# Seven-product chunk pairs in both feed-forwards, with the weight sums chained in place

## Chip, cores and metric

The kernel runs on one core of one Trainium2 chip, as one program. The time is that of the device for one execution, in microseconds; before the change the median of three runs was 784.88 us (784.01 to 785.82).

The engines are named as in the profile: PE is TensorE, PEld its weight loads, DVE VectorE, ACT ScalarE, POOL GpSimd, SP the engine whose queue issues most transfers ("SPq").

## What is computed

One layer of a streaming encoder over 256 tokens of 1024 values: a feed-forward, a mixer with two branches, a memory read, and a second feed-forward. The change touches the two feed-forwards only:

```python
def swiglu(h, w_in, w_down):
    gate, up = jnp.split(h @ w_in, 2, axis=-1)
    return (jax.nn.silu(gate) * up) @ w_down

h = rmsnorm(x, ffn1_pre_g[l])
x = x + 0.5 * rmsnorm(swiglu(h, ffn1_w_in[l], ffn1_w_down[l]), ffn1_post_g[l])
...
h = rmsnorm(x, ffn2_pre_g[l])
x = x + 0.5 * rmsnorm(swiglu(h, ffn2_w_in[l], ffn2_w_down[l]), ffn2_post_g[l])
```

`w_in` is 1024 x 5632 (gate and up of 2816 each), `w_down` 2816 x 1024, all in float32.

## The kernel before

**Precision.** A float32 operand is split into hi, a cast to float32r by ScalarE (`S.copy`), and lo, the rest, by a subtraction on VectorE. A product is three matmul passes: hi by hi, hi by lo, lo by hi. So each weight unit (128 x 1024, 512 KB) is loaded by SP into a tile "raw" of a ring of four, cast by ScalarE and subtracted by VectorE into a hi and a lo tile of rings of eight (`load_split`, L136-L148).

**A feed-forward** (`ffn`, L419) cuts the 2816 hidden columns into 11 chunks of 256. Each has four units of `w_in`, of which each covers a quarter of the 1024 inputs and holds gate and up columns, and two units of `w_down`. The input projection of a chunk is done in one of three ways:

- by token (`act_tok`, `act_first`), chunks 0 and 1, and 2 in the first feed-forward: the tokens are the stationary operand, 128 at a time, and the result must be transposed afterwards (`flush`, L427: four transposes, then a split of the result)
- by column (`act_col`, L457), most of the others: 128 weight columns are stationary; 32 matmuls of 512 columns and 32 of 256 per chunk; no transpose. Its results go through banks "mm" and "tr" of two each
- as a pair of chunks (`act_pair`, L545), before the change only in the second feed-forward, chunks 5 and 6, and 9 and 10

**A pair** treats tokens (two blocks of 128), inputs (two halves of 512) and chunks (two) as a 2 x 2 by 2 x 2 block product, done with seven block products in place of eight. B00 to B11 are the weight blocks: first index the half of the inputs, second the chunk; each is two units. A block product (`product`, L562) is 12 matmuls of 512 columns. Sums of token blocks (`pair_inputs`, L506: de, aed, ad, baed, and e) are made once a feed-forward, after chunk 2; they need a row of per-token factors that POOL fetches through memory (`row_of`). Sums of weight blocks are made by VectorE in the weight tiles (`add`, L541-L543): B00 + B01, B11 + B01, and from these two more. Before, all eight tiles of a pair are loaded ahead (`raw_loads`, L533), four into the pool "m4" of 21 tiles and four into the pool "extra" of four; the order is b0, b0's second part, b2, b3, b4, b1, b4's second part. Both chunks of a pair need transposes.

**The down projection** of a chunk (`down`, L489) is done in two halves (row blocks of 128 tokens, h = 0 and 1) of 12 matmuls each, and lags behind: the loop at L691 does what is due after each chunk, `STAG` = 3 chunks are left for the end. In a pair, halves are set between the products by `step_between` (L569), from a list made at L658: in the second feed-forward four halves (chunks 3 and 4) in pair 5, none in pair 9.

**Order.** Each engine runs its instructions in the order of its queue. A planner sets the order when the kernel is built: by program order, changed by `tc.high_priority()`, by `tc.issue_after(i)` (behind instruction i) and by `after(n)` (behind the n-th matmul). Tiles of a pool come free when the last reader is done.

The tiles of "extra" also hold the mixer's first weights (`place`, L776-L777).

Of the kernel before, what the change touches and what calls it, by code (L numbers as in the profile page):

```python
# [11 lines left out]
F32 = mybir.dt.float32  # L12
# [6 lines left out]
P = 128  # L19
# [13 lines left out]

STAG = 3

PAIRS = {"f1_in": (), "f2_in": (5, 9)}

L_ACT = 21
L_F1 = 24
# [41 lines left out]
def block_kernel(ctx: ExitStack, tc: tile.TileContext, wts, head_in, gf_in, x_in, mem_in, memT_in, cols, rows, fbias, masks, out):  # L81
# [36 lines left out]
    def mm():  # L118
        return pp.tile([P, 512], F32, tag="mm", name=nm("mm"), bufs=2)
# [299 lines left out]
    def ffn(w_in, w_dn, X, r2, n_tok, i_row, first_half, second_half=None):  # L419
# [110 lines left out]
                out[n] = t  # L530
            return out, q

        def raw_loads(c, k, n):  # L533
            t = []
            for j in range(2):
                r = wp.tile([P, D], F32, tag="extra", name=nm("sraw"), bufs=4) if n else m4([P, D], n="sraw")
                loads.append(nc.sync.dma_start(r, wts[_AT[w_in] + 4 * (c + n) + 2 * k + j - 4]).ins)
                t.append(r)
            return t

        def add(t, o):  # L541
            for x, y in zip(t, o):
                V.tensor_tensor(out=x, in0=x, in1=y, op=ALU.add)  # L543

        def act_pair(c, between):  # L545
            sx, q = pairs_in

            def of(n):
                return lambda kk: (sx[n][:, 0, kk], sx[n][:, 1, kk])

            def of_x(k):
                return lambda kk: (X.hi(4 * k + kk, 0, P), X.lo(4 * k + kk, 0, P))

            def splits(t):
                u = []
# [4 lines left out]
                return u  # L560

            def product(ps, stat, u, start):  # L562
# [36 lines left out]
            product(b4, of("ad"), splits(B01), True)  # L599
            step_between()  # L600
            b1 = trp()
            product(b1, of("aed"), splits(B11), True)
            with tc.high_priority():
                V.tensor_tensor(out=v, in0=p1, in1=b1, op=ALU.subtract)
                V.tensor_tensor(out=w, in0=b3, in1=v, op=ALU.subtract)  # L605
                t = half_tile("c11")
                V.tensor_tensor(out=t, in0=w, in1=b4, op=ALU.subtract)
                act_evac(t, c + 1, 1, r2[0], q)
                t = half_tile("c01")
                V.tensor_tensor(out=t, in0=w, in1=p3, op=ALU.add)  # L610
                act_evac(t, c + 1, 0)
            step_between()
            product(b4, of("e"), splits(B10), False)
            t = half_tile("c10")
            V.tensor_tensor(out=t, in0=v, in1=b4, op=ALU.add)
            silu = act_evac(t, c, 1, r2[0], q)
            if c + 1 == NFF - 1:
                table(silu)
            while between:
                step_between()  # L620

        def pair_loads(c):
            if c in pairs and c not in raws:
                raws[c] = [raw_loads(c, k, n) for k, n in ((0, 0), (1, 1), (0, 1), (1, 0))]

        raws = {}
# [21 lines left out]
        for c in range(n_tok, NFF):  # L648
            if c - 1 in pairs:
                continue  # L650
            if c > 2 and c not in pairs:
                pair_loads(c + 1)
            if c in pairs:
                pair_loads(c)
            acts[c] = m4([P, 2, 2, T], F32R, "act")
            if c in pairs:
                acts[c + 1] = m4([P, 2, 2, T], F32R, "act")
                downs = [(i, h) for i in range(done, min(c, NFF - STAG - 1)) for h in range(2)]  # L658
                done = max(done, min(c, NFF - STAG - 1))

                def one(i, h):
                    n = len(log)
                    down(i, h)
                    if h == 1:
                        flush(n + L_ACT - 12)

                act_pair(c, [lambda i=i, h=h: one(i, h) for i, h in downs])
            elif c == 2 and first_half:
                n = len(log)
                (outs,) = act_first((c,), mm)  # L670
                for h in range(2):
                    flush(n + L_ACT + 24 * h)
                    act_evac(outs[h], c, h)
            else:
                n = len(log)
                up = act_col(c)
                flush(n + L_ACT)
                flush(n + L_ACT + 20)
                split(acts[c][:, 0], acts[c][:, 1], up)
            last = c + 1 if c in pairs else c  # L680
            if c <= 6 <= last:
                grow = load_row(i_row)
                if first_half:
                    with tc.issue_after(loads[-1]):
                        nc.sync.dma_start(masks_s, masks)
# [851 lines left out]
```

## Time and profile before

| | us |
|---|---|
| median of three runs | 784.88 |
| lowest, highest | 784.01, 785.82 |
| the profiled execution | 785.81 |
| its span, first to last instruction | 784.0 |
| granted TensorE clock, mean | 0.997 |

| engine | busy us | share of the span |
|---|---|---|
| PE | 771.9 | 98% |
| DVE | 598.6 | 76% |
| ACT | 479.6 | 61% |
| POOL | 15.8 | 2% |

A timeline row has the start, the length, the engine, the line, the operation, the tile written and those read, shapes and a count; in brackets the idle time before it and what ended it. Neighbouring like rows are merged, and consecutive ones overlap a little at their ends, so that the distance of two starts is the cost of one in a row. In a row of stretches the numbers are: length, then busy time and count of PE, PEld, DVE, ACT, POOL, the granted clock, the busy share of the transfer engines and GB/s. A group row has a count, the busy time and mean ns, and the idle time before. Every matmul has line 95, that of its helper, so matmuls are told apart by tile: "acc" with "act" is the down projection, "mm" or "tr" with "hlT" the input projection, "sx" a pair's product with a sum of token blocks, "sraw" a weight block of a pair.

### The profile page before, as it was taken

The numbers are of one execution on the slowest core, as the hardware profiler recorded it, in microseconds if no ns is written. First come the engines' busy times: TensorE is split into PE (matmuls) and PEld (weight loads), VectorE is DVE, ScalarE is ACT, GpSimd is POOL, SyncE is SP. The second block draws the span as 40 slices with busy tenths as digits, with TensorE's granted clock in tenths as the row PEclk, the third lists the DMA queues.
The fourth block names the chain that finished last, engine by engine and source line by source line (L and its number), as shares of the span: only waits on it lengthen the run. The fifth ranks groups of instructions, "written<-read, shape, count | busy, mean of one in ns | idle before, by whom it ended". The sixth has DMA issues, their size and how long they took to land.

```text
span 784.0 us, 12029 instructions
## 1 busy us (share of the span) xinstructions
PE 771.9 (98%) x4526; PEld 660.6 (84%) x4526; DVE 598.6 (76%) x948; ACT 479.6 (61%) x798; POOL 15.8 (2%) x39
## 2 busy tenths in 40 slices
PE   9999999999999999999999999999999999999996
PEld 7888888888888998898788888888888888888775
DVE  7766656677778899788776666885589599986994
ACT  7665544567775668557676345753668566655852
POOL 0000000000000101100000000000000000000000
PEclk9999999999999999999999999999999999999998
DMA  9766665463654535834676654455175736286031
GB/s 347 258 228 204 224 217 190 162 235 137 215 172 145 181 137 172 286 109 162 214 260 230 215 183 163 147 204 191 54 259 173 273 135 273 93 293 254 0 108 54
DMA packets 44505, 148.07 MB, mean 189 GB/s; under 512 B 5144, under 2 KB 8864, under 8 KB 44448
## 3 DMA queue, kind: packets, MB, share of 16 engines
q1 hardware_dynamic: 43168, 144.83, 52.4%
q0 software_dynamic: 848, 2.12, 1.1%
q8 instruction: 35, 0.57, 0.3%
q10 hardware_dynamic: 432, 0.37, 0.1%
q14 instruction: 22, 0.18, 0.1%
HBM read 146.24 MB, written 1.06 MB: 188 GB/s over the span
## 4 chain that ended last, share of the span: by engine, by line
PE 87%; DVE 6%; DMA 3%; ACT 2%; issue 1%; DVEq 0%; ACTq 0%; SPq 0%
PE acc L95 37%; PE mm L95 36%; PE tr L95 11%; DMA raw<-in_wts_dram 2%; DVE lo L147 2%; DVE lo L166 2%; ACT hi L145 1%; DVE sraw L543 1%; PE tr L377 1%; PE tr L436 1%; ACT p L1162 0%; DMA head<-in_head_dram 0%; PE tr L1174 0%; DVE mx L1160 0%; DVE p L1159 0%
## 5 line engine op out<-in xcount | busy, mean ns | idle before, releaser
L147 DVE TENSOR_TENSOR lo<-raw,hi 128x1024 fp32r<-128x1024 f32 (+1 forms) x236 | 280.2, 1202 | 61.9 <-ACT hi L145 47.0
L145 ACT CAST hi<-raw 128x1024 fp32r<-128x1024 f32 (+1 forms) x236 | 239.7, 1036 | 87.8 <-DMA raw<-in_wts_dram 40.4
L95 PE MATMUL mm<-hi,hlT 128*128 128x512 f32 (+1 forms) x512 | 153.9, 379 | 0.0
L95 PE MATMUL acc<-hi,act 128*128 128x512 f32 x352 | 112.0, 391 | 0.0
L95 PEld LDWEIGHTS mm<-hi,hlT 128*128 128x128 f32 x512 | 94.2, 188 | 15.9 <-ACT pc L583 0.3
L95 PE MATMUL mm<-lo,hlT 128*128 128x512 f32 (+1 forms) x256 | 95.7, 379 | 0.0
L95 PEld LDWEIGHTS acc<-hi,act 128*128 128x128 f32 x352 | 66.1, 188 | 14.0 <-ACT act L165 0.5
L95 PE MATMUL mm<-hlT,hi 128*128 128x512 f32 (+1 forms) x320 | 76.5, 371 | 1.0 <-DVE at L444 0.6
L95 PE MATMUL acc<-lo,act 128*128 128x512 f32 x176 | 69.0, 392 | 0.2 <-DVE lo L147 0.2
L95 PE MATMUL acc<-hlT,hi 128*128 128x512 f32 x272 | 68.4, 393 | 0.0
L95 PEld LDWEIGHTS mm<-hlT,hi 128*128 128x128 f32 x320 | 56.6, 189 | 10.4 <-DVE vw L605 0.9
L95 PE MATMUL tr<-hlT,hi 128*128 128x512 f32 x240 | 60.3, 392 | 0.0
L95 PEld LDWEIGHTS acc<-hlT,hi 128*128 128x128 f32 x272 | 48.9, 189 | 8.8
L95 PEld LDWEIGHTS mm<-lo,hlT 128*128 128x128 f32 x256 | 48.0, 188 | 7.5
L95 PEld LDWEIGHTS tr<-hlT,hi 128*128 128x128 f32 x240 | 43.1, 189 | 7.7
L95 PE MATMUL mm<-hlT,lo 128*128 128x256 f32 x288 | 45.9, 284 | 0.0
L95 PEld LDWEIGHTS mm<-hlT,lo 128*128 128x128 f32 x288 | 41.4, 190 | 2.7
L95 PEld LDWEIGHTS acc<-hlT,lo 128*128 128x128 f32 x272 | 37.3, 190 | 2.7
L95 PEld LDWEIGHTS acc<-lo,act 128*128 128x128 f32 x176 | 33.1, 188 | 6.8 <-DVE lo L147 0.6
L95 PE MATMUL acc<-hlT,lo 128*128 128x256 f32 x272 | 38.6, 283 | 0.0
L166 DVE TENSOR_TENSOR lo<-sraw,hi 128x1024 fp32r<-128x1024 f32 x28 | 32.9, 1218 | 4.4 <-ACT hi L165 4.4
L95 PEld LDWEIGHTS tr<-hlT,lo 128*128 128x128 f32 x240 | 32.8, 190 | 2.3
(291 smaller groups left out, 1151.3 us busy)
## 6 DMA issues: line engine op xcount, KB each, us to landing
raw<-in_wts_dram SPq DMA_DIRECT2D x231, 512.0 KB, 4.4
sraw<-in_wts_dram SPq DMA_DIRECT2D x16, 512.0 KB, 6.0
raw<-in_gf_dram SPq DMA_DIRECT2D x12, 344.0 KB, 3.8
head<-in_head_dram SPq DMA_DIRECT2D x7, 392.0 KB, 6.6
grow<-in_rows_dram SPq DMA_DIRECT2D x4, 512.0 KB, 6.2
xs<-in_x_dram SPq DMA_DIRECT2D x2, 512.0 KB, 7.8
cbm<-cd POOLq DMA_DIRECT2D x2, 512.0 KB, 8.9
brow<-in_rows_dram SPq DMA_DIRECT2D x4, 256.0 KB, 3.8
```

Source lines behind the costliest of these rows:

```text
L95: log.append(PE.matmul(*args, **kw).ins)
L145: S.copy(h, r)
L147: V.tensor_tensor(out=l, in0=r, in1=h.bitcast(F32), op=ALU.subtract)
L166: b = V.tensor_tensor(out=lo, in0=src, in1=hi.bitcast(F32), op=ALU.subtract)
L377: PE.transpose(blocks[-1][1], src(kb), ident)
L436: PE.transpose(trv[:, j, h * P : (h + 1) * P], ats[c, h][:, j * P : (j + 1) * P], ident)
L543: V.tensor_tensor(out=x, in0=x, in1=y, op=ALU.add)
```

## The change

- `PAIRS`: chunks 6 and 7, and 9 and 10, in both feed-forwards. The first had no pairs; the second had 5 and 6, and 9 and 10.
- Weight blocks: B00 and B01 are loaded ahead into the four tiles of "extra" (`sums` and `both`), each behind the loads of the chunk before; B11 and B10 come during the pair through the ring of four raw tiles. No tile of "m4" holds weights any more.
- The sums are chained in place: `sums` becomes B00 + B01, then + B11, then + B10; `both` becomes B01 + B11. There are eight additions of a tile, as before.
- The order of products is b0, b2, b3, b1, b0's second part, b4, b4's second part. b3 takes a bank of "tr" in place of "mm".
- Six places for down halves in a pair instead of five, and the down of chunk c - 2 is held back before a pair: pair 6 has the halves of chunks 3, 4 and 5, pair 9 those of chunk 6.
- The evacuations of a pair have high priority; the transposes of the chunk after a pair stand 24 matmuls later, and a second group 16 behind the first instead of 20.

The argument `op` of `more` is always `None`, and of `halves` only the first entry is read.

```diff
-PAIRS = {"f1_in": (), "f2_in": (5, 9)}
+PAIRS = {"f1_in": (6, 9), "f2_in": (6, 9)}
...
+        def sum_load(c, n, halves):
             t = []
             for j in range(2):
-                r = wp.tile([P, D], F32, tag="extra", name=nm("sraw"), bufs=4) if n else m4([P, D], n="sraw")
-                loads.append(nc.sync.dma_start(r, wts[_AT[w_in] + 4 * (c + n) + 2 * k + j - 4]).ins)
+                r = wp.tile([P, D], F32, tag="extra", name=nm("sraw"), bufs=4)
+                more(r, c, *halves[0], j, None)
                 t.append(r)
             return t
...
+        def more(r, c, k, n, j, op):
+            src = wts[_AT[w_in] + 4 * (c + n) + 2 * k + j - 4]
+            if op is None:
+                loads.append(nc.sync.dma_start(r, src).ins)
+            else:
+                G.dma_start(r, src, accum_op=op)
...
+            def raws(k, n):
+                t = [wp.tile([P, D], F32, tag="raw", name=nm("raw"), bufs=4) for _ in range(2)]
+                for j in range(2):
+                    more(t[j], c, k, n, j, None)
+                return t
...
-            B00, B11, B01, B10 = raws.pop(c)
-            b0 = mm()
-            product(b0, of_x(0), splits(B00), True)
-            add(B00, B01)
+            sums, both = sums_of_pair.pop(c)
...
+            b0 = mm()
+            product(b0, of_x(0), splits(sums), True)
             S.copy(p1, b0)
             step_between()
-            product(b0, of_x(1), splits(B10), False)
-            act_evac(b0, c, 0)
             b2 = trp()
-            u = splits(B11)
-            add(B01, B11)
-            add(B11, B00)
-            add(B10, B11)
-            product(b2, of("baed"), u, True)
+            raw = raws(1, 1)
+            product(b2, of("baed"), splits(raw), True)
             S.copy(p3, b2)
             step_between()
-            b3 = mm()
-            product(b3, of("de"), splits(B00), True)
-            step_between()
-            b4 = mm()
-            product(b4, of("ad"), splits(B01), True)
+            add(sums, both)
+            add(both, raw)
+            b3 = trp()
+            product(b3, of("de"), splits(sums), True)
+            add(sums, raw)
             step_between()
             b1 = trp()
-            product(b1, of("aed"), splits(B11), True)
+            product(b1, of("aed"), splits(sums), True)
             with tc.high_priority():
                 V.tensor_tensor(out=v, in0=p1, in1=b1, op=ALU.subtract)
                 V.tensor_tensor(out=w, in0=b3, in1=v, op=ALU.subtract)
+            step_between()
+            raw = raws(1, 0)
+            product(b0, of_x(1), splits(raw), False)
+            with tc.high_priority():
+                act_evac(b0, c, 0)
+            add(sums, raw)
+            step_between()
+            b4 = mm()
+            product(b4, of("ad"), splits(both), True)
+            with tc.high_priority():
...
-            product(b4, of("e"), splits(B10), False)
+            product(b4, of("e"), splits(sums), False)
...
+            if c in pairs and c not in sums_of_pair:
+                with tc.issue_after(loads[-1]):
+                    sums_of_pair[c] = sum_load(c, 0, ((0, 0), (0, 1))), sum_load(c, 1, ((0, 1), (1, 1)))
...
-            if c > 2 and c not in pairs:
-                pair_loads(c + 1)
...
-                flush(n + L_ACT)
-                flush(n + L_ACT + 20)
+                wait = 24 if c - 2 in pairs else 0
+                flush(n + L_ACT + wait)
+                flush(n + L_ACT + wait + 16)
                 split(acts[c][:, 0], acts[c][:, 1], up)
             last = c + 1 if c in pairs else c
+            if c > 2 and c not in pairs:
+                pair_loads(c + 1)
...
-            while done < (NFF - STAG if last == NFF - 1 else min(c - 1, NFF - STAG - 1)):
+            while done < (NFF - STAG if last == NFF - 1 else min(c - 1 - (c + 1 in pairs), NFF - STAG - 1)):
```

More of the change, by code (lines that the diff above doesn't have):

```diff
@@ L531, in pair_inputs @@
             return out, q
-        def raw_loads(c, k, n):
+        def sum_load(c, n, halves):
             t = []
             for j in range(2):
-                r = wp.tile([P, D], F32, tag="extra", name=nm("sraw"), bufs=4) if n else m4([P, D], n="sraw")
-                loads.append(nc.sync.dma_start(r, wts[_AT[w_in] + 4 * (c + n) + 2 * k + j - 4]).ins)
+                r = wp.tile([P, D], F32, tag="extra", name=nm("sraw"), bufs=4)
+                more(r, c, *halves[0], j, None)
                 t.append(r)
             return t
-        def add(t, o):
-            for x, y in zip(t, o):
-                V.tensor_tensor(out=x, in0=x, in1=y, op=ALU.add)
+        def more(r, c, k, n, j, op):
[4 more added lines that the diff above has]
+                G.dma_start(r, src, accum_op=op)
         def act_pair(c, between):
@@ L560, in splits, with add @@
                 return u
+            def raws(k, n):
[3 more added lines that the diff above has]
+                return t
+            def add(t, o):
+                for x, y in zip(t, o):
+                    V.tensor_tensor(out=x, in0=x, in1=y, op=ALU.add)
             def product(ps, stat, u, start):
@@ L612, in act_pair @@
             step_between()
-            product(b4, of("e"), splits(B10), False)
-            t = half_tile("c10")
-            V.tensor_tensor(out=t, in0=v, in1=b4, op=ALU.add)
-            silu = act_evac(t, c, 1, r2[0], q)
+            product(b4, of("e"), splits(sums), False)
+            with tc.high_priority():
+                t = half_tile("c10")
+                V.tensor_tensor(out=t, in0=v, in1=b4, op=ALU.add)
+                silu = act_evac(t, c, 1, r2[0], q)
             if c + 1 == NFF - 1:
@@ L622, in pair_loads @@
         def pair_loads(c):
-            if c in pairs and c not in raws:
-                raws[c] = [raw_loads(c, k, n) for k, n in ((0, 0), (1, 1), (0, 1), (1, 0))]
-        raws = {}
+            if c in pairs and c not in sums_of_pair:
+                with tc.issue_after(loads[-1]):
+                    sums_of_pair[c] = sum_load(c, 0, ((0, 0), (0, 1))), sum_load(c, 1, ((0, 1), (1, 1)))
+        sums_of_pair = {}
         pairs, pairs_in = PAIRS[w_in], None
```

## The prediction

> **What bounds the kernel now.** I read the page first (busy shares, then the chain that ended last), then the chain in order of time, then single engines over the two feed-forwards, called FF1 and FF2 below.
>
> ```profile
> PE 771.9 (98%) x4526; PEld 660.6 (84%) x4526; DVE 598.6 (76%) x948; ACT 479.6 (61%) x798; POOL 15.8 (2%) x39
> ...
> PE 87%; DVE 6%; DMA 3%; ACT 2%; issue 1%; DVEq 0%; ACTq 0%; SPq 0%
> ```
>
> TensorE is busy nearly all the time and holds 87% of the chain, so a change pays through TensorE's work or its pauses. The chain in order of time (start, length, what) gives the prices:
>
> ```profile
> 61.66 5.56 PE mm L95 x32
> 67.22 5.59 PE tr L95 x32
> 72.81 5.47 PE acc L95 x24
> 78.27 5.56 PE mm L95 x32
> ...
> 667.54 2.72 PE mm L95 x12
> 670.26 2.72 PE acc L95 x12
> ```
>
> In FF1 a chunk's input projection takes 72.81 - 61.66 = 11.15 us, its down projection (24 matmuls) 5.46, and the next follows without a pause. In FF2's pair a block product of 12 matmuls takes 2.72, a down half of 12 the same: 0.227 us a matmul. Four transposes add 0.44 us (44.61 - 43.94, less one matmul):
>
> ```profile
> 43.94 0.60 PE L436 MATMUL tr<-ident,at 128*128 128x128 f32 x4
> 44.30 0.48 PE L95 MATMUL acc<-lo,act 128*128 128x512 f32 x1
> 44.61 0.40 PE L95 MATMUL acc<-hi,act 128*128 128x512 f32 x1
> ```
>
> FF2 from its first pair on does pause. PE rows, its first and last matmul of that stretch and the longest pause:
>
> ```profile
> 667.38 0.39 PE L95 MATMUL mm<-hi,hlT 128*128 128x512 f32 x1
> ...
> 760.11 0.88 PE L436 MATMUL tr<-ident,at 128*128 128x128 f32 x6 [0.81 <-DVE at L444]
> ...
> 776.64 0.39 PE L95 MATMUL acc<-hi,act 128*128 128x512 f32 x1
> ```
>
> In between lie two pairs (168 matmuls), 16 down halves (192), two column chunks (22.30) and four groups of transposes (1.76): 360 x 0.2267 + 24.06 = 105.67 us. It took 776.64 + 0.23 - 667.38 = 109.49, so 3.8 us are pauses.
>
> VectorE, which makes every lo half and every weight sum, is the one that could take over (stretch, then busy time):
>
> ```profile
> 45.00:62.00 17.00, 17.00 (x92) 14.61 (x91) 12.42 (x16) 9.86 (x14) 0.00 (x0) 1.00 0.60 201
> 62.00:78.00 16.00, 16.00 (x87) 13.84 (x86) 9.88 (x13) 8.32 (x12) 0.00 (x0) 1.00 0.56 188
> 628.00:667.00 39.00, 39.00 (x207) 33.57 (x206) 38.38 (x52) 23.78 (x35) 0.00 (x0) 1.00 0.55 210
> 714.00:764.00 50.00, 48.60 (x225) 39.36 (x225) 44.16 (x50) 29.28 (x37) 0.00 (x0) 1.00 0.30 110
> ```
>
> The third number after the stretch's length is DVE: 12.42 of 17 in FF1, but 38.38 of 39 in FF2 where the pair is prepared, with TensorE still at 39.00. A full VectorE need not stop TensorE, but leaves nothing over.
>
> **FF1's two pairs, on TensorE.** Removed: two column chunks a pair, 22.30 us. Added: seven products, 19.04, and two groups of transposes, 0.88. Each pair saves 2.38, the two 4.76. FF2 keeps two pairs, so its work there stays and only its 3.8 us of pauses can shrink.
>
> **FF1's two pairs, on VectorE.** Prices:
>
> ```profile
> 741.85 8.02 DVE L166 TENSOR_TENSOR lo<-sraw,hi 128x1024 fp32r<-128x1024 f32 x7
> ...
> L543 DVE TENSOR_TENSOR sraw<-sraw,sraw 128x1024 f32<-128x1024 f32 x16 | 18.9, 1218 | 0.1
> ...
> 630.83 0.94 DVE L508 RECIPROCAL rho<-row 128x128 f32<-128x128 f32 x1
> ...
> 643.13 2.49 DVE L166 TENSOR_TENSOR sx<-ss,sx 128x512 fp32r<-128x512 f32 x4
> ...
> 49.04 0.42 DVE L219 TENSOR_TENSOR gate<-mm,plo 128x256 f32<-128x256 f32 x1
> ```
>
> A full-tile subtraction or sum costs 1.14 us in a row (8.02 over 7; the sums have the same mean of 1218 ns), a half-size one 0.6 (2.49 over 4), a quarter 0.33 (a row's 0.42 less the 0.08 by which neighbours overlap). A pair needs 14 lo's and 8 sums, 25.1; two chunks needed 8 lo's, 9.1. Evacuations fall from 6.3 (per chunk four quarters, three half-size) to 5.6 (five and two half-size, four quarter ones at about 0.4 less overlap). So each pair adds about 15.3 us. The stationary sums of L506-L530, new in FF1, are 15 half-size operations and 1.1 us of small ones: 10.1.
>
> **Where these 10.1 us fall.** They come after chunk 2, where FF1 has its weights just in time:
>
> ```profile
> 44.92 2.36 DVE L147 TENSOR_TENSOR lo<-raw,hi 128x1024 fp32r<-128x1024 f32 x2 [1.10 <-ACT hi L145]
> ```
>
> and on TensorE and POOL
>
> ```profile
> 44.84 2.01 PE L95 MATMUL mm<-hlT,hi 128*128 128x512 f32 x8
> 46.70 1.11 PE L95 MATMUL mm<-hlT,lo 128*128 128x256 f32 x8
> ...
> 26.14 0.57 POOL L356 DMA_DIRECT2D row<-rd x1 [1.73 <-DMA rd<-runs]
> ...
> row<-rd POOLq DMA_DIRECT2D x4, 128.0 KB, 5.5
> ```
>
> A column chunk needs its lo's 1.86 us after its start. From 44.9 to chunk 4's need (61.66 + 1.86 = 63.5) DVE has 18.6 us; due are two down lo's 2.3, the split of chunk 2's activations 0.6, chunk 3's evacuations 3.1 and chunk 4's lo's 4.6: 10.6, with the new work 20.7, 2.1 too much. The row that they need lands near 31.7 (26.14 + 5.5), so some can go into idle gaps before 44.9, and b2 of the pair, their first reader, comes near 94 us, so some can go later. FF2 took the same 10.1 us without a pause (38.38 of 39). If they stand ahead of chunk 3's lo's, about half (5.7) is late; if in the gaps, nothing. Between 0 and 5.7 I take 1.0, nearer FF2's row.
>
> **Pair 6 in either feed-forward.** TensorE: 19.04 + six halves 16.3 = 35.4 us. VectorE: 25.1 + six down lo's 6.8 + 5.6 + chunk 8's lo's 4.6 = 42.1, of which the first lo's, the first sum and B11's lo's (6.8) can run beside chunk 5: 35.3 in 35.4. With a half behind each product TensorE takes 5.44 a step. Before each product the demand, summed from the pair's start (down lo's, sums, product lo's), stays under the supply: 6.8 by b3 at 10.9, 13.7 by b1 at 16.3, 24 by b4 at 27.2. So no pause there, from 0 to the 0.81 of the row at 760.11: the last half (down 5, second row block) holds the transposes of chunk 7, nine matmuls (2.0 us) after that chunk's last subtraction can start, and the evacuation takes some 2.5. I take 0.5.
>
> **Pair 9.** Only down 6 is left to put between, so three products in a row (b3, b1, b0's second part) want 2 lo's and 2 sums each, 4.56 us of DVE against 2.72 of PE. Chunk 8 and the pair give TensorE 11.15 + 0.44 + 24.5 = 36.1 us; VectorE owes the pair's 25.1, down 6's 2.3, chunk 8's 3.1, a split of transposes 0.6 and the pair's evacuations before their transposes 4.0, in all 35.1, and about 1.2 of pair 6's evacuation. What stalls is what was not done beside chunk 8. Before, pair 9 with down 7 among its products ran 732.48 to 758.24, 25.76 for 24.5:
>
> ```profile
> 732.48 0.39 PE L95 MATMUL mm<-hi,hlT 128*128 128x512 f32 x1
> ...
> 749.83 1.07 PE L95 MATMUL acc<-hi,act 128*128 128x512 f32 x4
> ...
> 758.24 0.61 PE L95 MATMUL acc<-hi,act 128*128 128x512 f32 x2
> ```
>
> That is 1.3 of pause, the lower bound being 0, the upper 3 x (4.56 - 2.72) = 5.5, if nothing is done early. I take 1.5, next to the measured 1.3.
>
> **After pair 9.** Of the 3.8 us, 1.4 came behind 758.24 (72 matmuls and 0.88 of transposes from there would end at 775.45 instead of 776.87). ScalarE had the activation of chunk 10's first half behind a weight cast that waited for a transfer:
>
> ```profile
> 758.14 1.05 ACT L145 CAST hi<-raw 128x1024 fp32r<-128x1024 f32 x1 [2.48 <-DMA raw<-in_wts_dram]
> 759.10 0.50 ACT L441 ACTIVATE sg<-c,facs 128x256 f32<-128x256 f32 x1
> ```
>
> The new code raises these evacuations' priority, and they end before b4's second part. I take 0.3 (0 to 1.4).
>
> **Costed at nothing.** The second product into b4 must wait until DVE has read the first (0.6 us); a half covers it in pair 6, matmuls of down 7 in pair 9, as at 749.83; uncovered, about 1 us a pair. B11's and B10's loads now sit in SP's queue and in the ring of four raw tiles, B11 holding two through b3; behind them on SP wait the loads of downs 4 and 5 and chunk 8. In FF2 SP waits for a slot, not for bandwidth, and a sum's load lands 6.0 us after issue, against 5.4 us for each product with its half:
>
> ```profile
> SPq L143 <- DVE lo L147: 115.0, 33, 33.7
> ...
> sraw<-in_wts_dram SPq DMA_DIRECT2D x16, 512.0 KB, 6.0
> ```
>
> Without that cover one load late costs up to 6.0 less the work at hand. The flushes that move by a few matmuls change no count.
>
> **The sum.** FF1: -4.76 + 1.0 + 0.5 + 1.5 + 0.3 = -1.5. FF2: 0.5 + 1.5 + 0.3 - 3.8 = -1.5. Together -3.0. The profiled execution took 785.81 (span 784.0 and 1.8 around it), which becomes 782.8; it lies 0.93 above the median of 784.88, so the median becomes **781.9**.
>
> **Rivals.**
> *All hidden.* Every pause vanishes: -4.76 - 3.8, 776.3. For it: FF2's 39 us at a full VectorE. Against: pair 9 has no reserve.
> *VectorE takes over in pair 9* (slower). Each in-place sum waits for the lo's of the tile it overwrites, these for a free hi/lo pair, and that for TensorE; so nothing runs ahead. Per feed-forward 5.5, with 0.8 and 1.4 at their bounds and 1.0 in FF1: FF1 +3.9, FF2 +3.9, so 792.7. It decides once pair 9 loses more than 3.0 us in each, which takes DVE some 3 us behind at chunk 8's end.
> *FF1's stationary sums come first*: 5.7 for 1.0, 786.6.
> *The halves don't do what they are there for*: TensorE's order draws them ahead of the products, pair 6 meets the demand of pair 9, and some 3 us more over both give 784.9, no change. For it: down 7 slid between products at 749.83.
> *A pause long enough to lower the clock.* In the last row here TensorE has nothing to do and the granted clock falls to 0.64; eight warm-up matmuls (two records each) took 3.65 us before the first real one, against 0.09 for a transpose of that size:
>
> ```profile
> 777.00:784.00 7.00, 0.03 (x1) 0.00 (x0) 2.74 (x7) 1.54 (x5) 0.00 (x0) 0.64 0.22 75
> ...
> 0.79 3.65 PE L95 MATMUL tr<-const-float32-1.0 128*128 128x128 f32 x16 [0.79 <-PEq L1526]
> ```
>
> If pair 9's 5.5 came as one pause, a like stretch of 3.65 at about half speed adds 1.8 to the 792.7: 794.5. Nothing so far pauses over 0.81, and 714 to 764 shows a clock of 1.00. The Trainium skill ("TensorE: Matmul & The Clock Gate", What's actually happening) puts the fall to half clock at an idle window of about 3.4 us. By that rule the three shortfalls of 1.84, one by one, would not trip it; the last row's fall agrees with it, and no row here shows so long a pause inside the kernel.
>
> **How the numbers follow.** Forecast 0.40 (its own range 779 to 784), all hidden 0.13, VectorE 0.18, stationary sums 0.12, halves 0.14, clock 0.03. About 0.2% (1.6 us) can be told from no change, so faster is below 783.3, slower above 786.5. Faster: 0.38 + 0.13 + 0.02 of the halves = 0.53. Same: 0.02 + 0.10 + 0.05 of the stationary sums = 0.17. Slower: 0.18 + 0.03 + 0.07 + 0.02 = 0.30. Range 776 to 789: it leaves out the clock and most of the VectorE case.
>
> **What would show it.** The mixer's first matmul after FF1 starting 1 to 4 us earlier; pairs of 84 matmuls in both; a pause of 1 to 2 us in each pair 9, named after a lo or a sum. Wrong if chunk 4 in FF1 waits for lo's beyond 3 us, if pair 6 pauses more than pair 9, or if FF2 has more than 3.8 us of pauses.

## The result, and the profile after

The changed kernel takes 780.78 us (median of 4 runs, 779.74 to 781.5), the kernel before 785.24 (4 runs, 784.01 to 785.82): a ratio of 0.9944, 95% interval 0.9926 to 0.9962, so 4.5 us faster. The forecast was 781.9. The total is close to it, its parts are not, so that its closeness is in part luck. Three stretches of TensorE, told apart by the first matmul of FF1, of the mixer ("mm<-w") and of FF2 (again "mm<-w"), and by the end of the span. Their rows before:

```profile
189.58 2.88 PE L95 MATMUL mm<-w,hlT 128*128 128x512 f32 x12
...
268.00 0.72 PE L95 MATMUL acc<-qf,early 128*32 128x32 f32 x59 [1.28 <-issue]
...
593.10 2.88 PE L95 MATMUL mm<-w,hlT 128*128 128x512 f32 x12
```

And after:

```profile
4.26 1.59 PE L95 MATMUL acc<-hi,hlT 128*128 128x512 f32 x4
...
184.69 2.88 PE L95 MATMUL mm<-w,hlT 128*128 128x512 f32 x12
...
267.67 0.42 PE L95 MATMUL mm<-hi,hlT 128*128 128x344 f32 x1 [3.38 <-issue]
...
591.22 2.88 PE L95 MATMUL mm<-w,hlT 128*128 128x512 f32 x12
```

| profiled execution, us | before | after | difference |
|---|---|---|---|
| up to FF1's first matmul | 4.58 | 4.26 | -0.3 |
| FF1, to the mixer's first matmul | 185.0 | 180.4 | -4.6 |
| mixer, to FF2's first matmul | 403.5 | 406.5 | +3.0 |
| FF2, to the end of the span | 190.9 | 186.3 | -4.6 |
| span | 784.0 | 777.5 | -6.5 |
| the execution | 785.81 | 779.74 | -6.1 |

Both feed-forwards gained 4.6 us, and the mixer, of which the change touches no line, lost 3.0. (The profiled execution after is the fastest of its four, that of before the slowest of its first three, which is why 6.1 stands here and 4.5 above.)

The busy line, the chain and the whole list of TensorE's waits after:

```profile
PE 766.7 (99%) x4454; PEld 656.2 (84%) x4454; DVE 636.9 (82%) x989; ACT 490.4 (63%) x807; POOL 16.0 (2%) x39
...
PE 99%; issue 1%; DVE 0%; DVEq 0%; ACT 0%; ACTq 0%
```

```profile
PE mm L95 <- issue: 3.4, 1, 3.4
PE tr L95 <- PEq L1546: 0.8, 1, 0.8
```

TensorE now holds 99% of the chain, for 87% before. VectorE has 38 us more to do (598.6 to 636.9), and yet no wait for it is left: the one at 0.8 is the kernel's start, the one of 3.4 lies in the mixer and names no engine. TensorE's records fell by 72, 36 for each of FF1's pairs.

Around pair 9 of both feed-forwards, where the pauses were forecast (length, then busy time of PE, PEld, DVE, ACT, POOL, clock):

```profile
136.50:162.84 26.34, 26.34 (x117) 21.54 (x116) 26.31 (x29) 17.45 (x23) 0.00 (x0) 1.00 0.30 106
```

```profile
711.78:723.40 11.62, 11.62 (x69) 10.14 (x69) 11.19 (x16) 5.44 (x10) 0.00 (x0) 1.00 0.37 138
723.40:749.74 26.34, 26.34 (x116) 21.50 (x116) 26.31 (x29) 17.54 (x23) 0.00 (x0) 1.00 0.31 105
```

VectorE is full to 0.03 us, and TensorE is full as well. The chain in order of time shows how, in FF1's pair 9:

```profile
147.41 5.44 PE tr L95 x24
152.85 5.44 PE mm L95 x24
158.29 1.80 PE acc L95 x7
160.09 2.72 PE mm L95 x12
```

The seven "acc" at 158.29 are matmuls of down 7 that slid in ahead of the last product.

### The profile page after: what moved, and what is told of

Read it like the earlier page. It is cut to its first block, busy times and chain, and to the rows that moved or that the text cites. A ratio compares the mean times of both kernels' runs of the same rounds, so it can differ in the third digit from the quotient of the medians.

```text
span 777.5 us, 11945 instructions
## 1 busy us (share of the span) xinstructions
PE 766.7 (99%) x4454; PEld 656.2 (84%) x4454; DVE 636.9 (82%) x989; ACT 490.4 (63%) x807; POOL 16.0 (2%) x39
## 4 chain that ended last, share of the span: by engine, by line
PE 99%; issue 1%; DVE 0%; DVEq 0%; ACT 0%; ACTq 0%
PE mm L95 43%; PE acc L95 40%; PE tr L95 13%; PE tr L377 1%; PE tr L436 1%; PE tr L1194 0%; PE tr L1288 0%; PE acc L1407 0%; DVE xs L413 0%; DVE post L408 0%; DVEq L1552 0%; ACT junk L285 0%; DVE t L320 0%; PE tr L1045 0%; DVE y L322 0%
## 5 line engine op out<-in xcount | busy, mean ns | idle before, releaser
L147 DVE TENSOR_TENSOR lo<-raw,hi 128x1024 fp32r<-128x1024 f32 (+1 forms) x220 | 261.1, 1202 | 43.8 <-ACT hi L145 37.7
L145 ACT CAST hi<-raw 128x1024 fp32r<-128x1024 f32 (+1 forms) x220 | 223.7, 1035 | 76.2 <-PE mm L95 37.4
L95 PE MATMUL mm<-hi,hlT 128*128 128x512 f32 (+1 forms) x544 | 165.9, 382 | 3.4 <-issue 3.4
L95 PE MATMUL mm<-hlT,hi 128*128 128x512 f32 (+1 forms) x256 | 60.1, 365 | 0.0
L165 ACT CAST hi<-sraw 128x1024 fp32r<-128x1024 f32 x40 | 41.5, 1054 | 16.6 <-DVE sraw L573 10.7
L95 PEld LDWEIGHTS mm<-hlT,hi 128*128 128x128 f32 x256 | 44.9, 189 | 6.5
L166 DVE TENSOR_TENSOR lo<-sraw,hi 128x1024 fp32r<-128x1024 f32 x40 | 48.4, 1218 | 0.1
L95 PE MATMUL tr<-hlT,hi 128*128 128x512 f32 x176 | 44.6, 393 | 0.0
L95 PE MATMUL mm<-hlT,lo 128*128 128x256 f32 x224 | 36.6, 284 | 0.0
L95 PEld LDWEIGHTS tr<-hlT,hi 128*128 128x128 f32 x176 | 31.5, 189 | 5.6
```

The lines of the kernel that those rows point to most:

```text
L95: log.append(PE.matmul(*args, **kw).ins)
L145: S.copy(h, r)
L147: V.tensor_tensor(out=l, in0=r, in1=h.bitcast(F32), op=ALU.subtract)
L165: a = S.copy(hi, src)
L166: b = V.tensor_tensor(out=lo, in0=src, in1=hi.bitcast(F32), op=ALU.subtract)
```

## The experiments

Twelve kernels ran. For each, from its profiled execution: FF1 from its first down matmul ("acc<-hi,act") to the mixer's first, which leaves out the first 39 us with their uneven warm-up; the mixer; FF2 to the span's end; and the pause in the mixer that names no engine.

| run | median us | FF1 | mixer | FF2 | that pause |
|---|---|---|---|---|---|
| before | 785.24 | 150.7 | 403.5 | 190.9 | 1.28 |
| after | 780.78 | 146.1 | 406.5 | 186.3 | 3.38 |
| e1_ff2_only | 780.96 | 150.7 | 401.5 | 186.7 | none |
| e2_ff1_only | 785.78 | 146.6 | 405.5 | 190.7 | 2.63 |
| e3_shift72 | 777.99 | 147.2 | 404.1 | 186.3 | none |
| e4_shift36 | 783.42 | 146.6 | 407.3 | 186.3 | 3.74 |
| e5_shift72_short | 776.58 | 147.1 | 401.8 | 186.3 | none |
| e6_lo_twice | 787.95 (one run) | 150.4 | 406.9 | 188.8 | 2.82 |
| e7_no_hold | 786.44 | 149.4 | 406.4 | 190.0 | 2.85 |
| e8_no_priority | 781.51 | 146.4 | 406.7 | 186.6 | 3.24 |
| e9_old_pair | 797.01 | 154.9 | 403.8 | 201.2 | 1.77 |
| e10_before_short | 793.50 | 151.9 | 409.2 | 191.2 | 4.62 |
| e11_loads_first | 780.32 | 146.6 | 404.5 | 186.2 | 1.63 |
| e12_order_only | 786.13 | 149.5 | 406.1 | 188.9 | 2.35 |

The kernel before, run beside them, had medians of 785.2 (with e1 to e4), 784.8 (e5 to e8), 785.5 (e9 to e11) and 785.8 (e12). The stretches are read before the totals, since the mixer's pause changes with nearly every edit.

### Each feed-forward alone

```diff
-PAIRS = {"f1_in": (6, 9), "f2_in": (6, 9)}
+PAIRS = {"f1_in": (), "f2_in": (6, 9)}
```

> The changed code with no pairs in the first feed-forward (FF1), (6, 9) in the second (FF2). Theory A (read off the two traces): FF2 alone gives about 4.6 us, and the mixer, which then meets the same TensorE instructions ahead of it as before, keeps its pause of about 1.3 us near 267 us: 785.2 - 4.6, about 780.6, FF1 ending at about 189.6 us. Theory B (the prediction's sum): FF2 gives 1.5, so about 783.7.

```diff
-PAIRS = {"f1_in": (6, 9), "f2_in": (6, 9)}
+PAIRS = {"f1_in": (6, 9), "f2_in": ()}
```

> The changed code with (6, 9) in FF1 and no pairs in FF2. FF2 then has no pauses but 4.8 us more matmul work than with pairs, about what its pauses cost before (3.8 to 4.7). Theory A: FF1 ends 4.9 us earlier, and the mixer takes back 3 to 3.7 us in the pause near 264 us that names no waiting engine: about 783.5. Theory B: FF1 gives 1.5 and nothing is taken back later: 783.7, but with FF1 ending only 1.5 us earlier. The end of FF1 and the mixer's pause tell them apart.

FF2 alone: 780.96, ratio 0.9947 (0.9931 to 0.9964). Its FF2 is as short as after (186.7), FF1 as long as before (150.7), and the mixer has no pause, where Theory A had one of about 1.3 stay: its time of 780.6 came out near without that part of its reason. FF1 alone: 785.78, ratio 1.0004 (0.9989 to 1.002); FF1 is 4.1 shorter than before, but the mixer has a pause of 2.63 us and is 2.0 longer. So the feed-forwards gain separately, some 4 us each, and in the profiled execution the mixer takes back half of FF1's gain. The expectation of 783.5 for FF1 alone had counted such a loss already, and the profiled execution (783.87) is near it; the ten executions run from 782.74 to 787.77, and why their median is 2 us longer than the profiled one no trace shows.

### The same kernel with TensorE's instructions shifted

Extra warm-up matmuls ahead of everything move all that follows in TensorE's instruction stream, and change nothing behind them.

```diff
-    for _ in range(WARM):
+    for _ in range(5):
         MM(wps[:, :P], one, one, start=True, stop=True)
+    for _ in range(39):
+        MM(wps[:32, :32], one[:, :32], one[:, :32], start=True, stop=True)
```

> The changed kernel; of the eight warm-up matmuls before the first load lands, three are replaced by 39 small ones (128x32 by 32), so that TensorE's later instructions stand 72 matmul records (144 instructions with their weight loads) further on, as far as the kernel before had them. Theory A (the pause near 264 us comes where a block of TensorE's instructions ends inside the burst of small matmuls): the pause is 1.3 us again as before, the clock stays at 1.00, and the time falls by about 3 us to 777 to 778. Rival (the pause comes from transfers or from the earlier start of the mixer): it stays at 3.4 us and the time at 780.8.

```diff
-    for _ in range(WARM):
+    for _ in range(7):
         MM(wps[:, :P], one, one, start=True, stop=True)
+    for _ in range(19):
+        MM(wps[:32, :32], one[:, :32], one[:, :32], start=True, stop=True)
```

> As e3, with one warm-up matmul replaced by 19 small ones: 36 records (72 instructions) further on. Theory A: a pause of another length, between nothing and 3.4 us, at another matmul of the same burst, and a time between 776 and 781. Rival: pause 3.4 us at the same matmul, 780.8.

With 72 more records the pause is gone (Theory A had 1.3 us of it left), and the time is 777.99 us (0.9914, 0.9898 to 0.9929), although FF1 starts some 2 us later and the mixer waits 1.57 us for VectorE at another place (378.78). With 36 more the pause is 3.74 us and lies inside a burst of small matmuls, 783.42 us (0.998, 0.9969 to 0.9991), which is above the 776 to 781 of Theory A. The next run takes the 72 records without the later start:

```diff
-    for _ in range(WARM):
-        MM(wps[:, :P], one, one, start=True, stop=True)
+    for _ in range(44):
+        MM(wps[:32, :32], one[:, :32], one[:, :32], start=True, stop=True)
```

> The kernel after, with its 8 warm-up matmuls (16 records, 3.8 us) replaced by 44 of 32x32 (88 records, so again 72 more, but by 0.043 to 0.054 us a record only 3.8 to 4.7 us). Theory A (the mixer's pause of 3.38 us and the low clock behind it come from where the block of instructions ends, and the longer warm-up alone cost the run with 72 records its later start): no pause over 0.5 us near 265 us, the first matmul of FF1 at about 4.6 us and the mixer's at 184.7 to 185.5, and 776 to 777.5 us by the clock. Rival: small matmuls do not raise the clock in time, FF1 starts with matmuls at half speed, about 2 us lost, 778 to 779. Rival B (the pause follows the change itself, and it went with 72 records by the later start): the pause is back, 780.8.

**776.58 us**, 0.989 (0.9875 to 0.9904): the fastest of all, and 4.2 below the kernel after. Its window around the place of the pause, and that of the kernel after:

```profile
262.00:275.00 13.00, 13.00 (x263) 12.74 (x262) 12.38 (x25) 9.38 (x14) 2.66 (x12) 1.00 0.51 189
```

```profile
262.00:275.00 13.00, 9.62 (x105) 9.29 (x92) 7.79 (x17) 6.14 (x10) 2.65 (x12) 0.87 0.30 115
```

TensorE is busy all 13.00 us at a clock of 1.00, for 9.62 at 0.87. The mixer is 4.7 us shorter (406.5 to 401.8), though the pause was only 3.38: the rest went into matmuls at a lower clock, as rows of the kernel after show:

```profile
263.50 0.48 PE L95 MATMUL mm<-hi,hlT 128*128 128x344 f32 x2
263.81 0.32 PE L95 MATMUL mm<-lo,hlT 128*128 128x344 f32 x1
...
268.15 0.78 PE L95 MATMUL mm<-hi,hlT 128*128 128x344 f32 x2
268.73 0.49 PE L95 MATMUL mm<-lo,hlT 128*128 128x344 f32 x1
```

A pair took 0.31 us before the pause (263.81 - 263.50) and 0.58 behind it. The same shift was then given to the kernel before:

> The kernel before with the short warm-up matmuls (44 of 32x32 for 8 large ones, 72 more records). Theory A (the pause in the mixer is a matter of where a block of instructions ends, with or without the change): the pause of 1.28 us at 268 moves off the small matmuls or shrinks, mixer 401.5 to 402.5 us long for 403.5, and 782.5 to 783.5 us; the change is then worth 6 to 7 us, compared with 776.6. If the pause only moves to another matmul of the same burst: 784 to 786.5. Rival B (72 records help the kernel after alone): 784.8.

793.50 us, 1.0102 (1.0082 to 1.0123), against all that was expected: the pause did not shrink, it grew.

```profile
268.29 0.71 PE L95 MATMUL acc<-qf,early 128*32 128x32 f32 x59
273.62 0.32 PE L95 MATMUL acc<-qf,early 128*32 128x32 f32 x3 [4.62 <-issue]
```

The mixer lost 5.7 us (409.2 for 403.5); most of the rest is FF1, which started 0.9 later and had a pause of 1.03. So 72 records do not help as such: they took the pause away in one kernel and made it 3.3 us longer in the other. The place in the instruction stream bears on it (last section), but it is not all: the run with FF2's pairs alone comes to the mixer after as many records as the kernel before, and has no pause where that one has 1.28 us.

### VectorE's reserve

The first four lo's of one pair are computed twice: pair 9 in FF1, pair 6 in FF2.

```diff
                     split(p[0], p[1], r)
+                    if c == (9 if w_in == "f1_in" else 6) and dose:
+                        dose.pop()
+                        V.tensor_tensor(out=p[1], in0=r, in1=p[0].bitcast(F32), op=ALU.subtract)
                     u.append(p)
```

> The kernel after, with the first four lo's of one pair computed a second time (the same values; 4 x 1.14 = 4.6 us more of VectorE): in pair 9 of FF1, and in pair 6 of FF2. Theory A (VectorE has nothing left in pair 9, busy 26.27 of 26.30 us, and some 1.6 us in pair 6, busy 34.16 of 35.8): the mixer's first matmul moves from 184.7 to 188 to 189.3 with 3.5 to 4.6 us of pauses in pair 9, and FF2's pair 6 pauses by 2 to 3 us. Theory B (VectorE is merely kept full by work that it does ahead, and the down products slide in between): at most 1 us in pair 9 and none in pair 6.

FF1 is 4.2 us longer (150.4 for 146.1) for 4.6 us of work, FF2 2.5 (188.8 for 186.3). That is near Theory A at both places, in the one execution that there is, though less of it stands as a pause in the pairs than expected: 2.56 and 0.31 us in FF1's pair 9, 0.43 at the end of FF2's pair 6 and 0.80 and 0.33 behind it. The longest pause in FF1's pair 9 and the window over it:

```profile
156.79 0.39 PE L95 MATMUL mm<-hi,sx 128*128 128x512 f32 x1
159.74 0.50 PE L95 MATMUL mm<-lo,sx 128*128 128x512 f32 x1 [2.56 <-DVE lo L166]
```

```profile
157.00:160.00 3.00, 0.44 (x2) 0.26 (x2) 3.00 (x5) 2.71 (x4) 0.00 (x0) 1.00 0.69 212
```

Here TensorE has no down matmul to put in (the next stand at 162.37) and waits while VectorE is busy all 3.00 us. Taken as they are, 4.2 us for 4.6 leave pair 9 a reserve of 0.4 us; but FF1 varies from 146.1 to 147.2 us among the five kernels that differ only ahead of it or behind it (the kernel after, and the runs with FF1 alone and with shifted instructions), so the reserve is known to about a microsecond. Nor is all of a full VectorE need: in the kernel after, three lo's of later weights (L147, at 157.87, 160.20 and 161.74) are made inside the pair, and here they stand behind 164.21.

### The parts of the change, one by one

Without the hold-back:

```diff
-            while done < (NFF - STAG if last == NFF - 1 else min(c - 1 - (c + 1 in pairs), NFF - STAG - 1)):
+            while done < (NFF - STAG if last == NFF - 1 else min(c - 1, NFF - STAG - 1)):
```

> The kernel after, without the hold-back: chunk 8 and chunk 5 no longer keep a down product, so that pair 9 has none of the six second halves between its products and pair 6 fewer; the matmuls are the same. Theory A (the halves are what hides VectorE's 15.3 us in a pair): pauses of 1.5 to 4 us in each pair 9, the mixer's first matmul at 186 to 189, and 784 to 789 us. Theory B (VectorE works ahead on lo's, the order of the down products does not matter): no pause over 0.5 us in a pair, 780.8 us. The pause near 265 us stays either way.

786.44 us, 1.0018 (1.0005 to 1.003): the whole gain is gone. FF1 +3.2, FF2 +3.7. Its waits of TensorE, the longest first:

```profile
PE mm L95 <- issue: 2.8, 1, 2.8
PE mm L95 <- DVE c L633: 1.6, 2, 0.8
PE mm L95 <- DVE c L624: 0.8, 1, 0.8
...
PE mm L95 <- DVE at L444: 0.6, 1, 0.6
```

The pauses of 1.6 (two) and 0.8 name the pair's evacuations (c) and stand partly at the first matmuls of chunk 8, not only inside pair 9: VectorE is late through the pair and what comes after it waits. The 0.6 is another matter: it stands in FF2's chunk 2 (621.87), ahead of any pair. The listed ones add up to less than the 3.2 and 3.7; the rest is spread over gaps too small for the list.

Without the priorities on the evacuations (b0's, the two behind b4, and the last; the first of three like edits is shown):

```diff
-            with tc.high_priority():
-                act_evac(b0, c, 0)
+            act_evac(b0, c, 0)
```

> The kernel after, with the three evacuations of a pair (the one after the fourth product, the two after the sixth, the one after the last) at the common priority again; only the subtraction of v and w keeps its own. Theory A (the priority is what takes the tail behind pair 9 away): the last silu and its product come behind one or two lo's of 1.14 us, 1 to 1.4 us of pause after each pair 9, and 782 to 783.6 us. Theory B (the lo's are done by then): no change, 780.8 us.

781.51 us, 0.9953 (0.9938 to 0.9968), FF1 and FF2 within 0.3 us of the kernel after: Theory B. The loads of the next pair ahead of chunk 5's and 8's own:

```diff
+            if c > 2 and c not in pairs:
+                pair_loads(c + 1)
             if c in pairs:
                 pair_loads(c)
...
-            if c > 2 and c not in pairs:
-                pair_loads(c + 1)
```

> The kernel after, with the loads of the next pair's first sums again ahead of the weights of the chunk before it (chunks 5 and 8), as before the change; their sums then too. Theory A (four loads of 512 KB ahead of chunk 5's or 8's own weights hold up that chunk: in the kernel before, raw loads issued behind four sum loads were waited for at 619 us): 0.5 to 1.5 us of pauses in chunk 5 or 8 of each feed-forward, 781.5 to 784 us. Theory B (the weights are four blocks ahead): no pause in the feed-forwards, 780.8 us give or take the mixer's pause.

780.32 us, 0.9939 (0.9919 to 0.996), no pause in a feed-forward over 0.21: Theory B again. Now the other way round, the kernel before with only its pairs moved:

```diff
-PAIRS = {"f1_in": (), "f2_in": (5, 9)}
+PAIRS = {"f1_in": (6, 9), "f2_in": (6, 9)}
```

> The kernel before with only the pairs moved: 6 and 9 in both feed-forwards; the old order of block products, old sums, no hold-back, no down product kept for pair 9. Theory A (without the halves between, VectorE's sums set the pace, as without the hold-back): FF1 saves its 4.5 us of matmuls and loses 2 to 4 of them in pauses of the pairs, mixer's first matmul at 187 to 189; FF2 189 to 190.5 us from its first matmul to the end; 782 to 785 us with whatever pause the mixer then has. Theory B (where the pairs stand does it all): mixer at 185, FF2 186.3 us, 777 to 781 us. In both, FF2's pause at 619 us (0.63 us, behind four sum loads at 606.21) should go, as pair 6 needs no sums so early: if it stays, the pair's place is not its cause.

797.01 us, 1.015 (1.0112 to 1.0188), worse than either theory had it. In the profiled execution, the slowest of four at 801.33 (4.3 us above the median), FF1 is 4.3 longer than before, though it has 4.76 us less to multiply, and FF2 10.3 longer. The last pair's chain in FF2 shows VectorE setting the pace:

```profile
747.04 3.41 DVE lo L166 x3
750.45 5.68 DVE sraw L543 x5
756.13 0.25 DVE at L444
756.37 9.12 DVE lo L166 x8
```

Eighteen microseconds of sums and lo's in a row hold the chain; the old order asks for several sums together ahead of b3. At chunk 2 of FF2 the forecast of a vanishing pause failed too. The transfer queue's issues and TensorE's row:

```profile
611.14 2.16 SPq L537 DMA_DIRECT2D sraw<-in_wts_dram  x4
```

```profile
626.48 1.97 PE L95 MATMUL mm<-hlT,hi 128*128 128x512 f32 x6 [2.86 <-DVE at L444]
```

With the pair one chunk later its first sums were still loaded in chunk 2's time, and the pause was longer. So it wasn't the pair's place. The clock fell behind this pause, to 0.70:

```profile
626.40:632.00 5.60, 5.52 (x23) 4.75 (x24) 2.28 (x4) 2.16 (x4) 0.00 (x0) 0.70 0.53 196
```

and again around the waits in chunk 8 (0.66 from 725 to 735), so that a part of this run's loss is the clock. Last, the new order alone, with all else as before:

```diff
-                wait = 24 if c - 2 in pairs else 0
-                flush(n + L_ACT + wait)
-                flush(n + L_ACT + wait + 16)
+                flush(n + L_ACT)
+                flush(n + L_ACT + 20)
...
-            while done < (NFF - STAG if last == NFF - 1 else min(c - 1 - (c + 1 in pairs), NFF - STAG - 1)):
+            while done < (NFF - STAG if last == NFF - 1 else min(c - 1, NFF - STAG - 1)):
```

(with the loads' place of e11, and high priority only for v, w and the two evacuations behind b4, as before)

> The kernel after with all but the pair itself as before: the new order of block products with its sums in place in four tiles, pairs 6 and 9 in both; but no hold-back, the old flush distances, the loads' old place, and the two new priorities gone. The kernel before with the same pairs and its old order took 797.0 us (FF1 149.6 us from its first matmul to just before the mixer's less the 40 us ahead, i.e. the mixer's first at 194.2; FF2 201.2 us). Theory A (the order of products is the larger part: it asks for its sums later and needs its blocks one by one): about as the run without the hold-back, mixer's first matmul 188.5 to 190, FF2 189.5 to 191 us, 785 to 788 us; the order is then worth about 10 of the 16 us, the hold-back the other 6. Theory B (the flush distances and priorities carry it, each alone hides the other's absence): 790 to 797 us, with waits of the pairs for at, v or w over 2 us.

786.13 us, 1.0002 (0.9989 to 1.0014): Theory A, and FF1 and FF2 stand where the run without the hold-back has them (149.5 and 188.9 for 149.4 and 190.0, of which 0.6 is that run's pause in chunk 2). Its first sum loads in FF2 leave late:

```profile
649.77 0.42 SPq L544 DMA_DIRECT2D sraw<-in_wts_dram  x1
```

So of the 16 us between the old pair code (797.0) and the kernel after (780.8), the order of products, with its four tiles and the later loads that belong to it, is worth 10.9 (797.0 to 786.1; more in the feed-forwards, as e9's mixer is 2.3 us shorter; which of the three carries it was not tried) and the hold-back the remaining 5.4 to 5.7; the priorities, the loads' place and, as e7 and e12 agree, the flush distances are worth nothing that shows.

## Why the prediction was right or wrong

- **FF1's work on TensorE, -4.76.** Right: FF1 takes 4.6 us less.
- **Stationary sums in FF1, +1.0.** Nothing in the profiled execution after. They lie where the prediction's lower bound had them, in VectorE's gaps ahead of chunk 3 and on:

```profile
37.83 0.69 DVE L517 TENSOR_TENSOR xf<-hlT 128x512 f32<-128x512 f32 x1
...
53.33 0.68 DVE L166 TENSOR_TENSOR sx<-xf,sx 128x512 fp32r<-128x512 f32 x1
```

The gaps are not always enough: in e3, e5 and e9 chunk 3 waits 0.82, 0.55 and 0.88 us for a split that stands behind four lo's of these sums. The rows of e5:

```profile
52.59 2.50 DVE L166 TENSOR_TENSOR sx<-ss,sx 128x512 fp32r<-128x512 f32 x4
```

```profile
55.84 2.09 PE L95 MATMUL tr<-hlT,hi 128*128 128x512 f32 x8 [0.55 <-DVE act L166]
```

(The upper bound of 5.7 has no working in the prediction; half of 10.1 is 5.05.)

- **Pair 6, +0.5, and pair 9, +1.5.** Nothing in either feed-forward. The balance in pair 9 was near enough: 36.3 us of VectorE were forecast for chunk 8 and the pair, the rows have 11.19 + 26.31 = 37.5 in 37.96. The step that failed is the one from the balance to a pause: "I take 1.5, next to the measured 1.3". The 1.3 was measured with the old order, which asks for several sums together and which without the hold-back is 10.9 us slower than the new one (e9, e12). In the new order a full VectorE does not stop TensorE while there are down matmuls to slide in, and there are about enough: 4.6 us more of VectorE cost 4.2 (e6).
- **After pair 9, 0.3 left of 1.4.** All of it went, but not by the priority that I gave as the reason: without it nothing comes back (e8).
- **FF2's pauses, -1.5 net.** FF2 gained 4.6. All 3.8 us of pauses went, and some 0.9 came in a stretch that the sum did not look at, up to the end of chunk 2, where the kernel before had issued four sum loads early. The windows up to there, before and after:

```profile
593.10:634.31 41.21, 40.58 (x202) 34.22 (x201) 30.36 (x62) 27.40 (x50) 1.17 (x2) 1.00 0.62 219
```

```profile
591.22:631.56 40.34, 40.34 (x202) 34.12 (x201) 30.64 (x62) 27.83 (x50) 1.17 (x2) 1.00 0.49 171
```

and the issues and the pause before:

```profile
606.21 2.16 SPq L537 DMA_DIRECT2D sraw<-in_wts_dram  x4
...
611.51 19.43 SPq L143 DMA_DIRECT2D raw<-in_wts_dram  x8
```

```profile
619.33 1.65 PE L95 MATMUL mm<-hlT,hi 128*128 128x512 f32 x6 [0.63 <-DVE at L444]
```

After, the first sum load leaves at 652.64. That the later loads cure it is not shown. For it: the three runs with the early loads pause here (before 0.63, e9 2.86, e10 1.09 us), and most with the later ones do not (e12 among them). Against it: the run without the hold-back (e7) issues no sum load in this stretch, and pauses all the same:

```profile
621.87 1.65 PE L95 MATMUL mm<-hlT,hi 128*128 128x512 f32 x6 [0.59 <-DVE at L444]
```

In both it is a cast on ScalarE that waits for a weight's transfer, 2.33 us before and 2.29 in e7, for 0.47 in the kernel after; why the transfer is late without a sum load ahead of it stays open.
- **The rest of the kernel, 0.** Wrong by 3.0: the mixer's pause grew from 1.28 to 3.38 us and the clock fell behind it. "Nothing so far pauses over 0.81" overlooked the 1.28 us in the trace before, and the prediction counted TensorE's records that go (36 a pair) only as time, not as a shift of the instruction stream. That the shift is what made the pause longer is likely, from the runs with shifted instructions, but not shown.

Two errors of opposite sign thus made the total: 6 us too little gained in the feed-forwards, 3 not seen in the mixer, and the rest lies between the profiled executions and the medians. That they nearly cancel is luck. **The rivals.** "All hidden" (776.3) is what both feed-forwards did; the kernel that has that and no pause in the mixer takes 776.58 (e5). That VectorE takes over is what the old order does (797.0) and what the new one is a microsecond or less away from (e6). "The halves don't do what they are there for" fell: without them between the products the gain is gone (e7). The clock did fall after a pause, in the kernel after only in the mixer and at a pause that names no engine; behind waits that name VectorE it fell in e9.

## What to carry to other kernels

A full helper engine is no pause as long as the main engine has other ready work between: look at what can slide in, and measure the reserve by doubling one of the helper's steps. Spread the sums so that each product asks for its own just before it; here the order that does this, with its tiles and loads, was worth twice the held-back work, and both were worth more than any priority. When a change alters the number of instructions, look for waits named "issue" far from it, read each stretch by itself, and try a shift of the stream before judging the total.

## What the hardware showed

- **A pause that no engine causes.** In all but three of the 14 kernels TensorE stops once between 263 and 276 us, for 1.28 to 4.62 us, inside the burst of small matmuls of the recurrence (before, e4, e10) or 1.8 to 1.9 us behind its end (the eight with FF1's pairs and the common warm-up). The burst after:

```profile
260.63 1.29 PE L95 MATMUL acc<-q,k 128*32 128x32 f32 x126
261.77 0.74 PE L95 MATMUL acc<-qf,early 128*32 128x32 f32 x62
```

That is 188 matmuls and as many weight loads in 1.9 us, about 200 records a microsecond, where the whole kernel has 2 x 4454 in 777.5, 11 a microsecond. A transfer queue of its own brings the instructions:

```profile
q8 instruction: 35, 0.57, 0.3%
```

Blocks of 0.016 MB each. The records do not say whose block it is; TensorE's 2 x 4454 records over 35 blocks would be some 254 a block, an estimate that takes all of them for TensorE's. Counted from the start of the program, TensorE stops at nearly one place: behind 1499 to 1502 matmuls in ten of the eleven kernels, and in e10 behind 1630, which is 131 matmuls or 262 records further. Stretches that end inside the pause, with TensorE's count in the first brackets, in the kernel after, e4 and e10:

```profile
0.00:267.00 267.00, 263.50 (x1499) 224.26 (x1499) 230.79 (x342) 176.95 (x276) 6.52 (x25) 1.00 0.61 214
```

```profile
0.00:267.20 267.20, 262.90 (x1499) 223.74 (x1500) 228.70 (x337) 176.77 (x275) 5.34 (x19) 1.00 0.62 213
```

```profile
0.00:273.30 273.30, 267.18 (x1630) 230.06 (x1630) 191.22 (x296) 164.90 (x266) 5.33 (x19) 1.00 0.62 209
```

So a shift of the stream changes which matmul stands at this place. Around the pause of the kernel after, blocks arrive in the half microseconds from 265.0 and 268.5, in e10 from 271.0 and 274.5; in all eleven kernels TensorE goes on 2.3 to 3.5 us behind the start of a half microsecond in which a block arrives. In the three that do not stop, a block arrives before the burst begins (e1 264.0 and 265.69, e3 261.5 and 263.51, e5 260.0 and 262.37). That TensorE had used up its instructions and waited for the next block fits all this; it is argued and not shown. The place alone does not decide: e1 passes it without a pause, and the kernel before, with as many records ahead and a block from 264.5 for a burst at 265.36, stops for 1.28 us. The Trainium skill ("Runtime: NRT & Kernel Launch", Instruction fetch mechanics) describes such blocks, fetched while the one before is executed, and calls the fetch hidden; if the pause is the fetch, these runs differ from it by up to 4.62 us.
- **The clock behind it.** It fell after pauses of 2.35 (e12), 2.82, 2.85, 3.24, 3.38, 3.74 and 4.62 us and not after 1.28, 1.63, 1.77 and 2.63 (e2); of the pauses in the feed-forwards it fell behind 2.86 (e9) and not behind 2.56 (e6, at 1.00 from 159.74 to 163). The window of e2 reads

```profile
262.00:275.00 13.00, 10.37 (x214) 10.04 (x204) 9.46 (x19) 7.64 (x13) 2.65 (x12) 1.00 0.38 141
```

so that no single length decides. The Trainium skill ("TensorE: Matmul & The Clock Gate", What's actually happening) has a window of about 3.4 us that runs freely, whatever the kernel does; that the length alone doesn't decide agrees with it, a fall after 2.35 us does not agree with a whole idle window.
- **The first matmuls.** The stretch of FF1 ahead of its first down matmul took 34.1 to 35.5 us in the kernels with the common warm-up, which are alike there: 34.3 after, 35.1 in e8. Differences of a microsecond at the start say nothing of a change behind it.
